# Block operands of a Strassen-Winograd up projection: stored ready for use, or made from stored h where they are used

## The chip, the cores and the metric

The kernel runs on one core of one Trainium2 chip. The metric is the device time of one execution in microseconds (us), the median of several runs. Five instruction streams work side by side and meet at semaphores: TensorE (PE, matmuls), VectorE (DVE), ScalarE (ACT), GpSimd (POOL) and SyncE (SP). SP and POOL here also issue the transfers between HBM and on-chip memory, each as a queue of its own in order of issue.

## The reference

One decoder layer on 2048 tokens of width 1024, all in fp32:

```
u   = x @ W_in                         # columns q | k | v | rnn-x | rnn-gate
att = sliding_window_attention(q, k, v, sinks)
rec = rg_lru(causal_conv(rnn-x)) * gelu(rnn-gate)
h   = LN1(alpha * x + concat(att, rec) @ W_out)
g, v = split(h @ W_up)                 # 2 x 3072 columns
ffn = (gelu(causal_conv3(g)) * v) @ W_down
ple = sigmoid(h @ W_g + b_g) * (p @ W_p)
out = LN2(alpha * h + ffn + ple)
```

## The kernel before

Every fp32 factor of a matmul is split into a high and a low half in a type that PE multiplies at a higher rate: ACT casts the high half and DVE subtracts it (`split_sb`, L122 to L124), and `mm3` (L140 to L143) sums three matmuls, high·high, high·low and low·high. Weights come as 512 KB blocks by SP into three buffers (wst) and are split into eight buffers of a pair of halves (wb). Transposed activations lie in 13 buffers of 1 MB (pool h).

The first part loops over four chunks c of 512 tokens. The input stage projects x (halves xh, xl) and runs attention and the recurrence. The gate stage is the output projection (`mh`, `ml`), LN1, transposes of h into halves hh, hl and an fp32 copy hf (L517 to L526), and the per-layer gate: small products of p (halves in `pt`, bank `a`) and the product h W_g (bank `acc`), put together by DVE and ACT (L588 to L592), and the row sums stored to `rsd` (L594).

The second part runs twice, s2 = 0 and 1, over a pair of chunks: `up(s2)` and `down(s2)`. up multiplies the 1024-wide h of both chunks with the up weights as a 2x2 block product by the Strassen-Winograd scheme: seven products in place of eight for each of 24 weight tiles ft. h's four blocks are B11 (chunk 2·s2, first 512 features), B21 (the same chunk, last 512), B12 and B22 (the next chunk). The operands are B11, T2 = B22 − B12 + B11, B21, T1 = B12 − B11, T3 = B22 − B12, T4 = B21 − T2 and B22, each as a high and a low half of four quarters kt. `begin(ft)` splits seven weight combinations and multiplies B11; `middle` does T2, B21 (which completes the gate block of the first chunk), T1 and T3; `end` does T4 and B22. PE's order in up is the order in the code; elsewhere a scheduler sets the order of all engines.

The operands go through HBM. In chunks 0 and 2 the halves of B11 and B21 are stored as they are (L537) beside fp32 hf (L538). In chunks 1 and 3, between the token blocks of the gate, `combine(kt)` (L543 to L557) fetches a quarter of B11 and B21 by SP into two rows of pool xb (L546, L547), makes the four sums on DVE (L549 to L552), splits them into pch and pcl, and stores the halves to hxT2, hxT1, hxT3, hxT4 by POOL (L556, L557). `load_hx` (L238 to L251) loads finished operands by POOL: for s2 = 0 in chunk 3 (L529, L600), for s2 = 1 in down(0) (L753, L772). xb has two buffers, which up also uses for the convolution rows (L653, L675).

x is loaded by SP through the wst buffers (L275 to L284), and so are the row constants (`load_rows`, L206).

Of the kernel before, what the change touches and what calls it, by code (L numbers as in the profile page):

```python
# [8 lines left out]
F32 = mybir.dt.float32  # L9
# [19 lines left out]
HX = ("B11", "T2", "B21", "T1", "T3", "T4", "B22")  # L29
# [11 lines left out]
def kernel(  # L41
# [196 lines left out]
    def load_hx(s2, names, earlier):  # L238

        for n in names:  # L240
            hx[s2][n] = []
            for m in range(2):
                if (n, m) == (HX[-1], 1):
                    ts = [tm(("pch", "pcl")[k % 2], F32R) for k in range(4)]
                    for k in range(4):
                        order(POOL.dma_start(f(ts[k]), hxd[s2][n][:, m, k, :]), earlier)
                else:
                    t = h8(n, [P, 4, T])
                    order(POOL.dma_start(f(t), hxd[s2][n][:, m]), earlier)
                    ts = [t[:, k, :] for k in range(4)]  # L250
                hx[s2][n].append(ts)  # L251

    for c in range(NCH):
# [21 lines left out]
        for u in range(c == 0, 4):  # L275
            if c == 0:
                st = tm("r", cols=1024)
            else:
                st = wst_p.tile([P, 1024], F32, tag="wst", name=nm("wst"))
            order(SP.dma_start(st.rearrange("p (k t) -> p k t", k=2), xt[c, :, 2 * u:2 * u + 2, :]), have_h)  # L280
            hi, lo = x_flat(u)
            for h in range(2 - (c > 0)):
                hs = slice(h * 512, 1024 if c else h * 512 + 512)
                split_sb(st[:, hs], hi[:, hs], lo[:, hs])  # L284
# [570 lines left out]
```

## Time and profile before

| | |
|---|---|
| median of 3 runs | 2374.26 us (2372.97 to 2375.92) |
| profiled execution | 2377.13 us, its span 2375.4 us |
| mean granted clock of PE | 0.987 of 2.4 GHz |
| PE busy | 2291.5 us, 96% of the span |
| DVE, ACT, POOL busy | 1653.0, 1084.5, 265.2 us |
| packets of SP's queue, of POOL's | 266.97 MB and 71.31 MB |

The span is the time from the first instruction to the last on the chip; the time of the execution is a little longer. Busy time says how long an engine worked, not whether the end waited for it. In a timeline row the brackets hold how long the engine stood idle before this instruction, and the instruction or the transfer that released it. In a row of windows, the number in brackets behind a busy time is the count of instructions, then follow the granted clock (1.00 is 2.4 GHz, 0.50 is 1.2 GHz), the share of time in which the core's transfer engines worked, and what they moved.

### The profile page before, as it was taken

How to read it: one execution, taken by the hardware profiler on the slowest of the kernel's cores; microseconds unless marked ns; L12 is line 12 of the kernel's file. 1: busy time of each engine (PE TensorE's matmuls, PEld its weight loads, DVE VectorE, ACT ScalarE, POOL GpSimd, SP SyncE). 2: the span in 40 equal slices, each digit the busy share in tenths (PEclk: the TensorE clock that was granted, in tenths of full speed). 3: DMA queues.
4: the chain of work that ended last, by engine and by line, in shares of the span. 5: the costliest groups of instructions: out<-in, count | busy, mean ns of one | idle time of the engine just before them, and what ended most of it. 6: DMA issues, size and time to landing. Idle time of an engine off the chain costs nothing.

```text
span 2375.4 us, 28589 instructions
## 1 busy us (share of the span) xinstructions
PE 2291.5 (96%) x10156; PEld 1871.1 (79%) x10156; DVE 1653.0 (70%) x2728; ACT 1084.5 (46%) x2030; POOL 265.2 (11%) x483
## 2 busy tenths in 40 slices
PE   8899999899999977999999999999999999999998
PEld 7777777677787756888888888878888888888886
DVE  6975787778778756777777753636877777753735
ACT  7644664566456443444444433333444444433331
POOL 0300130213003112001001000000000000000000
PEclk9999999999999988999999999999999999999999
DMA  4237324832542468222222264765322222254542
GB/s 161 98 108 262 119 80 168 293 115 74 213 165 90 170 238 326 85 80 87 87 80 82 92 208 133 271 238 201 117 86 80 85 80 83 90 193 153 194 158 83
DMA packets 102095, 340.11 MB, mean 143 GB/s; under 512 B 10944, under 2 KB 11072, under 8 KB 96576
## 3 DMA queue, kind: packets, MB, share of 16 engines
q1 hardware_dynamic: 87840, 266.97, 33.9%
q0 software_dynamic: 14112, 71.31, 7.6%
q8 instruction: 80, 1.31, 0.2%
q14 instruction: 63, 0.52, 0.1%
HBM read 262.74 MB, written 75.50 MB: 142 GB/s over the span
## 4 chain that ended last, share of the span: by engine, by line
PE 59%; DVE 2%; DMA 1%; ACT 0%; issue 0%; DVEq 0%; ACTq 0%
PE b L141 7%; PE b L143 7%; PE b L142 7%; PE acc L141 5%; PE acc L143 5%; PE acc L142 5%; PE a L141 5%; PE a L143 5%; PE a L142 5%; PE sc L143 2%; PE sc L142 2%; PE sc L141 2%; DMA wst<-in_w_dram 1%; DMA xb<-hfd 0%; DVE st L214 0%
## 5 line engine op out<-in xcount | busy, mean ns | idle before, releaser
L123 ACT CAST wb<-wst 128x512 fp32r<-128x512 f32 x640 | 391.9, 622 | 677.0 <-PE acc L143 321.3
L124 DVE TENSOR_TENSOR wb<-wst,wb 128x512 fp32r<-128x512 f32 x640 | 433.5, 686 | 277.4 <-ACT wb L123 276.6
L141 PE MATMUL b<-T,wb 128*128 128x512 f32 x576 | 225.5, 392 | 7.1 <-DMA T<-hxT 5.4
L142 PE MATMUL b<-T,wb 128*128 128x512 f32 x576 | 225.2, 391 | 1.9 <-DMA T<-hxT 1.9
L143 PE MATMUL b<-T,wb 128*128 128x512 f32 x576 | 225.1, 391 | 0.0
L123 ACT CAST wb<-xc 128x512 fp32r<-128x512 f32 x144 | 89.4, 621 | 199.1 <-PE a L143 94.5
L141 PE MATMUL a<-B,wb 128*128 128x512 f32 x384 | 149.6, 390 | 0.0
L142 PE MATMUL a<-B,wb 128*128 128x512 f32 x384 | 149.5, 389 | 0.0
L143 PE MATMUL a<-B,wb 128*128 128x512 f32 x384 | 149.4, 389 | 0.0
L124 DVE TENSOR_TENSOR wb<-xc,wb 128x512 fp32r<-128x512 f32 x144 | 99.1, 688 | 50.8 <-ACT wb L123 50.8
L141 PEld LDWEIGHTS b<-T,wb 128*128 128x128 f32 x576 | 108.6, 189 | 31.1 <-issue 5.8
L142 PEld LDWEIGHTS b<-T,wb 128*128 128x128 f32 x576 | 108.6, 189 | 24.9 <-DMA T<-hxT 2.4
L620 DVE SCALAR_TENSOR_TENSOR pl<-xb,prm,pl 128x512 f32<-128x512 f32 x96 | 71.8, 748 | 78.7 <-POOL xb L676 77.4
L143 PEld LDWEIGHTS b<-T,wb 128*128 128x128 f32 x576 | 108.7, 189 | 22.7
L141 PE MATMUL acc<-wb,hh 128*128 128x512 f32 x256 | 101.5, 401 | 11.4 <-DVE P L588 5.8
L143 PE MATMUL acc<-wb,hl 128*128 128x512 f32 x256 | 101.7, 399 | 1.7 <-DVE hl L99 1.7
L142 PE MATMUL acc<-wb,hh 128*128 128x512 f32 x256 | 102.3, 400 | 0.0
L142 PE MATMUL a<-xl,wb 128*128 128x512 f32 x256 | 101.0, 394 | 0.0
L141 PE MATMUL a<-xh,wb 128*128 128x512 f32 x256 | 100.7, 393 | 0.0
L143 PE MATMUL a<-xh,wb 128*128 128x512 f32 x256 | 100.6, 393 | 0.0
L141 PE MATMUL acc<-xh,wb 128*128 128x512 f32 x192 | 77.5, 403 | 8.0 <-ACT wb L123 7.5
L143 PEld LDWEIGHTS a<-B,wb 128*128 128x128 f32 x384 | 72.2, 188 | 15.1
(272 smaller groups left out, 5728.0 us busy)
## 6 DMA issues: line engine op xcount, KB each, us to landing
wst<-in_w_dram SPq DMA_DIRECT2D x319, 512.0 KB, 3.6
graw<-gd SPq DMA_DIRECT2D x24, 1024.0 KB, 6.4
T<-hxT POOLq DMA_DIRECT2D x16, 1024.0 KB, 9.8
gd<-pl SPq DMA_DIRECT2D x48, 256.0 KB, 2.0
gd<-r SPq DMA_DIRECT2D x48, 256.0 KB, 4.2
B<-hxB POOLq DMA_DIRECT2D x10, 1024.0 KB, 9.7
r<-in_xn_dram SPq DMA_DIRECT2D x16, 512.0 KB, 4.0
ln<-in_rows_dram SPq DMA_DIRECT2D x16, 512.0 KB, 4.5
```

What stands on the lines that cost most here:

```text
L123: ACT.copy(hi, src)
L124: (eng or DVE).tensor_tensor(lo, src, f(hi), ALU.subtract)
L141: order(PE.matmul(o, ah, bh, start=first, stop=False, skip_group_check=more), after)
L142: PE.matmul(o, ah, bl, start=False, stop=False, skip_group_check=more)
L143: return PE.matmul(o, al, bh, start=False, stop=last, skip_group_check=more)
L620: DVE.scalar_tensor_tensor(gc, xb[:, t_:t_ + T], pc(C_FW + 3 * ft + t_), gc, ALU.mult, ALU.add)
```

## The change

HBM keeps only hf, in fp32, as two halves of 1 MB for each of the four chunks. The operands are made where they are used. `combine(0, kt)` now runs in chunk 3's gate alone: POOL fetches a quarter of B11 (into an xb row), B12 (pch) and B22 (pcl); the split goes straight to tiles of pool h, which now stay. `combine(1, kt)` runs in down(0)'s second chunk. At the start of each up, `combine_b21` makes B21 and T4 from a fetched quarter and from T2's halves, and `combine_b22` makes B22. For the first tile the product with B21 stands behind those with T1 and T3. x is loaded by POOL as two tiles of 1 MB in pool h, and the row constants by POOL too. Lines of the changed kernel differ from those above.

```diff
-    hfd = [scratch(f"hfd{s}", [P, 8, T], F32) for s in range(2)]
+    hfd = [[scratch(f"hf{c}_{u}", [P, 4, T], F32) for u in range(2)] for c in range(NCH)]
     gd = [[scratch(f"gd{s}_{k}", [P, 4, 2 * T], F32) for k in range(NF // 4)] for s in range(2)]
-    hxd = [{n: scratch(f"hx{n}_{s}", [P, 2, 4, T], F32) for n in HX} for s in range(2)]
 
     def load_rows(i):
         t = tm("ln", cols=1024)
-        SP.dma_start(t, rows[i:i + 1].broadcast_to([P, 1024]))
+        POOL.dma_start(t, rows[i:i + 1].broadcast_to([P, 1024]))
...
-    def load_hx(s2, names, earlier):
...
+    def fetch(t, c, u, kt, earlier):
+        order(POOL.dma_start(t, hfd[c][u][:, kt, :]), earlier)
+        return t
+
+    def operands(s2, names):
         for n in names:
-            hx[s2][n] = []
-            for m in range(2):
-                if (n, m) == (HX[-1], 1):
-                    ts = [tm(("pch", "pcl")[k % 2], F32R) for k in range(4)]
-                    for k in range(4):
-                        order(POOL.dma_start(f(ts[k]), hxd[s2][n][:, m, k, :]), earlier)
-                else:
-                    t = h8(n, [P, 4, T])
-                    order(POOL.dma_start(f(t), hxd[s2][n][:, m]), earlier)
-                    ts = [t[:, k, :] for k in range(4)]
-                hx[s2][n].append(ts)
+            hx[s2][n] = [[t[:, k, :] for k in range(4)] for t in (h8(n, [P, 4, T]), h8(n, [P, 4, T]))]
+
+    def operand(s2, n, kt, src):
+        split_sb(src, hx[s2][n][0][kt], hx[s2][n][1][kt])
+
+    def combine(s2, kt, earlier):
+
+        if kt == 0:
+            operands(s2, ("B11", "T2", "T1", "T3"))
+        b11 = fetch(row()[:, 0:T], 2 * s2, 0, kt, earlier)
+        b12 = fetch(tm("pch"), 2 * s2 + 1, 0, kt, earlier)
+        b22 = fetch(tm("pcl"), 2 * s2 + 1, 1, kt, earlier)
+        t3, t1, t2 = (tm("xc") for _ in range(3))
+        DVE.tensor_tensor(t3, b22, b12, ALU.subtract)
+        operand(s2, "B11", kt, b11)
+        DVE.tensor_tensor(t2, t3, b11, ALU.add)
+        operand(s2, "T2", kt, t2)
+        DVE.tensor_tensor(t1, b12, b11, ALU.subtract)
+        operand(s2, "T1", kt, t1)
+        operand(s2, "T3", kt, t3)
+
+    def combine_b21(s2, kt, earlier):
+
+        if kt == 0:
+            operands(s2, ("B21", "T4"))
+        b21 = fetch(row()[:, 0:T], 2 * s2, 1, kt, earlier)
+        operand(s2, "B21", kt, b21)
+        t4 = tm("xd")
+        DVE.tensor_tensor(t4, f(hx[s2]["T2"][0][kt]), f(hx[s2]["T2"][1][kt]), ALU.add)
+        DVE.tensor_tensor(t4, b21, t4, ALU.subtract)
+        operand(s2, "T4", kt, t4)
+
+    def combine_b22(s2, earlier):
+        hi = h8("B22", [P, 4, T])
+        hx[s2]["B22"] = [[hi[:, k, :] for k in range(4)], [tm(("pch", "pcl")[k % 2], F32R) for k in range(4)]]
+        for kt in range(4):
+            operand(s2, "B22", kt, fetch(row()[:, 0:T], 2 * s2 + 1, 1, kt, earlier))
...
+        if c > 0:
+            for u in range(2):
+                st = h8("xs", [P, 4, T], F32)
+                order(POOL.dma_start(st, xt[c, :, 4 * u:4 * u + 4, :]), have_h)
+                for h in range(2):
+                    hi, lo = x_flat(2 * u + h)
+                    split_sb(st[:, 2 * h:2 * h + 2, :].rearrange("p k t -> p (k t)"), hi, lo)
...
-        if c == NCH - 1:
-            load_hx(0, HX[:1], last_scores)
-            load_hx(0, HX[1:3], [mixed])
...
-        if c % 2 == 0:
-            for u, n in enumerate(("B11", "B21")):
-                for m, t in enumerate((hh_[u], hl_[u])):
-                    POOL.dma_start(hxd[s2][n][:, m], f(t))
-                POOL.dma_start(hfd[s2][:, 4 * u:4 * u + 4], hf[u])
-        else:
-            for m, t in enumerate((hh_[1], hl_[1])):
-                POOL.dma_start(hxd[s2]["B22"][:, m], f(t))
-
...
-            SP.dma_start(b11, hfd[s2][:, kt, :])
-            SP.dma_start(b21, hfd[s2][:, 4 + kt, :])
-            t3, t1, t2, t4 = (tm(t) for t in ("xc", "xc", "xc", "xd"))
-            DVE.tensor_tensor(t3, b22, b12, ALU.subtract)
-            DVE.tensor_tensor(t1, b12, b11, ALU.subtract)
-            DVE.tensor_tensor(t2, t3, b11, ALU.add)
-            DVE.tensor_tensor(t4, b21, t2, ALU.subtract)
-            for n, t in (("T2", t2), ("T1", t1), ("T3", t3), ("T4", t4)):
-                hi, lo = tm("pch", F32R), tm("pcl", F32R)
-                split_sb(t, hi, lo)
-                POOL.dma_start(hxd[s2][n][:, 0, kt, :], f(hi))
-                POOL.dma_start(hxd[s2][n][:, 1, kt, :], f(lo))
+        for u in range(2):
+            POOL.dma_start(hfd[c][u], hf[u])
...
-                if c % 2 and t_ % 2 != dh:
-                    combine(2 * dh + t_ // 2)
-            if dh == 0:
-                half = [gated]
-        if c == NCH - 1:
-            load_hx(0, HX[3:6], half)
-            load_hx(0, HX[6:], [gated])
+                if c == NCH - 1 and t_ % 2 != dh:
+                    combine(0, 2 * dh + t_ // 2, last_scores)
+            ready_for_b21 = [gated]
...
+            def gate():
+                product(v["A"], w2, x["B21"], False)
...
+            if not first:
+                gate()
             product(v["C"], w5, x["T1"], True)
             product(v["B"], w7, x["T3"], False)
...
+            if first:
+                gate()
...
             v = begin(0)
-            middle(v)
+            for kt in range(4):
+                combine_b21(s2, kt, ready_for_b21)
+            middle(v, True)
+            combine_b22(s2, ready_for_b21)
...
+                if c == 1 and 3 < kp < 8:
+                    combine(1, kp - 4, marks[-1:])
...
-                    if c == 1:
-                        load_hx(1, HX[:4], marks[-1:])
...
-            if c == 1:
-                load_hx(1, HX[4:], marks[-2:-1])
...
-        down(s2)
+        ready_for_b21 = down(s2)
```

Three places show how instructions move. The first is POOL at the seam between chunk 3's gate and up(0). Before: rsd15 is the last row-sum store of the gate, the hx names are operands in HBM, gtail a small copy of the first tile's convolution.

```order
291 L594 DMA rsd15_117<-r_1363_7249 128x1024
292 L249 DMA T3_1553_8202<-hxT3_0_136 128x2048
293 L249 DMA T3_1554_8204<-hxT3_0_136 128x2048
294 L249 DMA T4_1555_8206<-hxT4_0_137 128x2048
295 L249 DMA T4_1556_8208<-hxT4_0_137 128x2048
296 L249 DMA B22_1557_8210<-hxB22_0_138 128x2048
297 L246 DMA pch_1558_8212<-hxB22_0_138 128x512
298 L246 DMA pcl_1559_8213<-hxB22_0_138 128x512
299 L246 DMA pch_1560_8214<-hxB22_0_138 128x512
300 L246 DMA pcl_1561_8215<-hxB22_0_138 128x512
301 L654 COPY xb_1579_8297<-gtail_100 128x2
```

After, from the last rsd stores on; hf0_1 is the second half of chunk 0's h in HBM (B21), hf1_1 that of chunk 1 (B22), ln a row constant.

```order
238 L237 DMA pch_1452_7909<-hf1_0_120 128x512
239 L598 DMA rsd12_114<-r_1298_7071 128x1024
240 L598 DMA rsd13_115<-r_1299_7073 128x1024
241 L598 DMA rsd14_116<-r_1300_7075 128x1024
242 L237 DMA xb_1477_8011<-hf0_1_119 128x512
243 L237 DMA xb_1479_8020<-hf0_1_119 128x512
244 L206 DMA ln_2057_11648<-in_rows_dram 128x1024
245 L598 DMA rsd15_117<-r_1301_7077 128x1024
246 L237 DMA xb_1481_8029<-hf0_1_119 128x512
247 L237 DMA xb_1483_8038<-hf0_1_119 128x512
248 L656 COPY xb_1490_8103<-gtail_100 128x2
249 L658 COPY gtail_100<-xb_1490_8103 128x2
```

Nine loads of whole operands and quarters behind the last rsd store are gone. Eight fetches of a quarter stand there instead, each into an xb row; two of them ahead of the last rsd store, four behind the small copies of the first tile.

The second place is DVE at the start of up(0). Before, the first tile's weight combinations (wb, wst, xc) follow the gate's last operations on row sums (P, r); ph is the first sum behind a product with T2.

```order
1244 L592 SCALAR_TENSOR_TENSOR r_1363_7249<-r_1363_7249,P_1550_8192 128x512
1245 L124 TENSOR_TENSOR wb_1570_8240<-xc_1564_8226,wb_1570_8240 128x512
1246 L633 TENSOR_TENSOR wst_1563_8224<-wst_1562_8222,wst_1563_8224 128x512
1247 L636 TENSOR_TENSOR xc_1566_8228<-wst_1562_8222,xc_1565_8227 128x512
1248 L651 TENSOR_TENSOR ph_1578_8283<-b_1576_8269,P_1575_8267 128x512
1249 L124 TENSOR_TENSOR wb_1571_8244<-wst_1563_8224,wb_1571_8244 128x512
1250 L124 TENSOR_TENSOR wb_1572_8247<-wst_1563_8224,wb_1572_8247 128x512
1251 L124 TENSOR_TENSOR wb_1573_8251<-xc_1566_8228,wb_1573_8251 128x512
1252 L124 TENSOR_TENSOR wb_1588_8342<-wst_1583_8334,wb_1588_8342 128x512
1253 L627 TENSOR_TENSOR xc_1585_8338<-wst_1584_8336 128x512
```

After, from the first B21 split on; B21 and T4 rows with L123 are low halves, L270 and L271 the sums for T4, and wb_1506 and up are weights of the second tile.

```order
1216 L123 TENSOR_TENSOR B21_1474_8008<-xb_1477_8011,B21_1473_8007 128x512
1217 L271 TENSOR_TENSOR xd_1478_8015<-xb_1477_8011,xd_1478_8015 128x512
1218 L123 TENSOR_TENSOR B21_1474_8008<-xb_1479_8020,B21_1473_8007 128x512
1219 L651 TENSOR_TENSOR ph_1487_8061<-b_1485_8047,P_1472_8005 128x512
1220 L123 TENSOR_TENSOR T4_1476_8010<-xd_1478_8015,T4_1475_8009 128x512
1221 L123 TENSOR_TENSOR wb_1506_8141<-wst_1501_8133,wb_1506_8141 128x512
1222 L270 TENSOR_TENSOR xd_1480_8024<-T2_1394_7612,T2_1395_7613 128x512
1223 L629 TENSOR_TENSOR xc_1504_8138<-xc_1503_8137,wst_1501_8133 128x512
1224 L271 TENSOR_TENSOR xd_1480_8024<-xb_1479_8020,xd_1480_8024 128x512
1225 L123 TENSOR_TENSOR B21_1474_8008<-xb_1481_8029,B21_1473_8007 128x512
1226 L123 TENSOR_TENSOR wb_1507_8145<-xc_1504_8138,wb_1507_8145 128x512
1227 L123 TENSOR_TENSOR T4_1476_8010<-xd_1480_8024,T4_1475_8009 128x512
```

Splits and sums of B21 and T4 now stand between the weights of the second tile, and in DVE's order a weight waits behind a quarter that is still to be fetched.

The third place is POOL in chunk 0's gate. Before, six stores of operands and hf, and then the stores of row sums, the next small copy behind them in the program's later part:

```order
58 L537 DMA hxB11_0_132<-hh_274_1603 128x2048
59 L537 DMA hxB11_0_132<-hl_276_1605 128x2048
60 L538 DMA hfd0_118<-hf_278_1607 128x2048
61 L537 DMA hxB21_0_134<-hh_275_1604 128x2048
62 L537 DMA hxB21_0_134<-hl_277_1606 128x2048
63 L538 DMA hfd0_118<-hf_279_1608 128x2048
64 L594 DMA rsd0_102<-r_236_1319 128x1024
65 L594 DMA rsd1_103<-r_237_1321 128x1024
```

After, with the loads of the next chunk's x (xs) and of row constants:

```order
59 L206 DMA ln_241_1321<-in_rows_dram 128x1024
60 L206 DMA ln_300_1707<-in_rows_dram 128x1024
61 L313 DMA xs_369_2114<-in_xt_dram 128x2048
62 L561 DMA hf0_0_118<-hf_278_1599 128x2048
63 L561 DMA hf0_1_119<-hf_279_1600 128x2048
64 L313 DMA xs_370_2120<-in_xt_dram 128x2048
65 L598 DMA rsd0_102<-r_236_1311 128x1024
```

Four stores went, two stores of hf stay, and the second half of x stands behind them on the same queue.

## Rows read from the trace of the kernel before

**Rows 1.** The page's first part: busy us, share of the span, instructions of each engine

```profile
PE 2291.5 (96%) x10156; PEld 1871.1 (79%) x10156; DVE 1653.0 (70%) x2728; ACT 1084.5 (46%) x2030; POOL 265.2 (11%) x483
```

**Rows 2.** Windows by stage: stretch, us, busy us by engine, clock, DMA share, GB/s

```profile
335.23:453.45 118.22, 110.04 (x482) 86.36 (x480) 93.15 (x141) 61.55 (x106) 23.93 (x44) 0.99 0.57 200
453.45:564.06 110.61, 102.20 (x477) 82.77 (x477) 91.24 (x183) 73.19 (x176) 26.65 (x40) 0.97 0.39 129
564.06:674.41 110.35, 107.38 (x481) 85.76 (x480) 79.69 (x118) 55.99 (x95) 11.07 (x19) 1.00 0.51 179
674.41:779.23 104.82, 100.06 (x477) 81.35 (x476) 85.99 (x169) 70.48 (x170) 24.76 (x36) 1.00 0.35 115
779.23:915.07 135.84, 116.66 (x482) 90.80 (x481) 92.84 (x143) 57.92 (x102) 27.30 (x50) 0.91 0.62 232
915.07:1385.49 470.42, 461.80 (x2021) 380.90 (x2020) 344.82 (x537) 197.07 (x323) 47.40 (x110) 0.99 0.33 107
1385.49:1647.68 262.19, 260.88 (x1150) 215.23 (x1148) 126.22 (x196) 84.68 (x149) 9.18 (x17) 1.00 0.59 210
1647.68:2106.26 458.58, 458.16 (x2022) 379.05 (x2021) 348.21 (x541) 195.65 (x320) 34.29 (x72) 1.00 0.30 99
```

**Rows 3.** PE timeline, gate stage of chunk 3: start, us, instruction, [idle before, releaser]

```profile
838.87 0.79 PE L141 MATMUL acc<-wb,hh 128*128 128x512 f32 x1 [4.53 <-ACT wb L123]
...
853.62 0.79 PE L141 MATMUL a<-wb,pt 128*128 128x512 f32 x1 [4.73 <-ACT pt L123]
...
858.49 0.79 PE L143 MATMUL a<-wb,pt 128*128 128x512 f32 x1 [3.65 <-DVE pt L124]
...
907.86 0.50 PE L141 MATMUL acc<-wb,hh 128*128 128x512 f32 x1 [3.55 <-DVE P L588]
```

**Rows 4.** DVE timeline, same stage

```profile
856.61 0.69 DVE L550 TENSOR_TENSOR xc<-hf,xb 128x512 f32<-128x512 f32 x1 [2.51 <-DMA xb<-hfd]
...
903.98 0.69 DVE L550 TENSOR_TENSOR xc<-hf,xb 128x512 f32<-128x512 f32 x1 [6.45 <-DMA xb<-hfd]
```

**Rows 5.** PE timeline, start of chunk 2's input stage

```profile
453.45 0.50 PE L141 MATMUL acc<-xh,wb 128*128 128x512 f32 x1 [2.14 <-ACT wb L123]
...
458.01 0.80 PE L143 MATMUL acc<-xh,wb 128*128 128x512 f32 x1 [3.83 <-DVE wb L124]
```

**Rows 6.** PE timeline, start of up(0)

```profile
931.49 0.77 PE L141 MATMUL b<-T,wb 128*128 128x512 f32 x1 [5.38 <-DMA T<-hxT]
...
943.62 0.50 PE L141 MATMUL b<-T,wb 128*128 128x512 f32 x1 [1.33 <-DVE xd L662]
```

**Rows 7.** Windows: late gate of chunk 3, start of up(0), start of up(1)

```profile
828.21:915.07 86.86, 68.58 (x274) 52.64 (x273) 55.61 (x88) 37.51 (x67) 19.54 (x37) 0.86 0.73 273
915.07:945.00 29.93, 21.30 (x79) 16.42 (x78) 16.61 (x28) 10.53 (x19) 8.76 (x17) 0.83 0.92 356
1647.68:1672.00 24.32, 24.32 (x109) 20.15 (x108) 23.80 (x39) 11.18 (x19) 1.83 (x4) 1.00 0.59 220
```

**Rows 8.** Groups by line: line, engine, operation, count, busy us, mean ns, idle before

```profile
L124 DVE TENSOR_TENSOR wb<-wst,wb 128x512 fp32r<-128x512 f32 x640 | 433.5, 686 | 277.4 <-ACT wb L123 276.6
...
L123 ACT CAST wb<-wst 128x512 fp32r<-128x512 f32 x640 | 391.9, 622 | 677.0 <-PE acc L143 321.3 <-PE b L143 192.3 <-DMA wst<-in_w_dram 70.0
...
L556 POOL DMA_DIRECT2D hxT<-pch x32 | 17.2, 540 | 58.0 <-ACT pch L123 57.8
```

**Rows 9.** DMA issues: name, queue, count, KB each, median us to landing

```profile
hxT<-pch POOLq DMA_DIRECT2D x32, 256.0 KB, 4.7
...
wst<-in_xt_dram SPq DMA_DIRECT2D x12, 512.0 KB, 4.3
...
hfd<-hf POOLq DMA_DIRECT2D x4, 1024.0 KB, 14.5
...
xb<-hfd SPq DMA_DIRECT2D x16, 256.0 KB, 5.8
...
pch<-hxB POOLq DMA_DIRECT2D x4, 256.0 KB, 12.2
```

More of the change, by code (lines that the diff above doesn't have):

```diff
@@ L27 @@
 EPS = 1e-5
-HX = ("B11", "T2", "B21", "T1", "T3", "T4", "B22")
 W_IN, W_OUT, W_UP, W_DOWN, W_PG, W_PP = 0, 14, 22, 70, 94, 102
@@ L274 @@
                 ready[W_IN + 6].append(wblock(st[1][:, hs]))
-        for u in range(c == 0, 4):
+        for u in range(1, 4):
             if c == 0:
                 st = tm("r", cols=1024)
-            else:
[L279 to L284, printed above, removed]
+                SP.dma_start(st.rearrange("p (k t) -> p k t", k=2), xt[c, :, 2 * u:2 * u + 2, :])
+                hi, lo = x_flat(u)
+                for h in range(2):
+                    hs = slice(h * 512, h * 512 + 512)
+                    split_sb(st[:, hs], hi[:, hs], lo[:, hs])
+        if c > 0:
+            for u in range(2):
+                st = h8("xs", [P, 4, T], F32)
+                order(POOL.dma_start(st, xt[c, :, 4 * u:4 * u + 4, :]), have_h)
+                for h in range(2):
+                    hi, lo = x_flat(2 * u + h)
+                    split_sb(st[:, 2 * h:2 * h + 2, :].rearrange("p k t -> p (k t)"), hi, lo)
         def first_stage(o, unit, bh, bl):
@@ L526 @@
                 ACT.copy(hf[u][:, :, t_ * P:(t_ + 1) * P], tpv)
-        if c == NCH - 1:
-            load_hx(0, HX[:1], last_scores)
-            load_hx(0, HX[1:3], [mixed])
-        s2 = c // 2
-        if c % 2 == 0:
-            for u, n in enumerate(("B11", "B21")):
-                for m, t in enumerate((hh_[u], hl_[u])):
-                    POOL.dma_start(hxd[s2][n][:, m], f(t))
-                POOL.dma_start(hfd[s2][:, 4 * u:4 * u + 4], hf[u])
-        else:
-            for m, t in enumerate((hh_[1], hl_[1])):
-                POOL.dma_start(hxd[s2]["B22"][:, m], f(t))
-        def combine(kt):
-            b12, b22 = hf[0][:, kt, :], hf[1][:, kt, :]
-            b11, b21 = row()[:, 0:T], row()[:, 0:T]
-            SP.dma_start(b11, hfd[s2][:, kt, :])
-            SP.dma_start(b21, hfd[s2][:, 4 + kt, :])
-            t3, t1, t2, t4 = (tm(t) for t in ("xc", "xc", "xc", "xd"))
-            DVE.tensor_tensor(t3, b22, b12, ALU.subtract)
-            DVE.tensor_tensor(t1, b12, b11, ALU.subtract)
-            DVE.tensor_tensor(t2, t3, b11, ALU.add)
-            DVE.tensor_tensor(t4, b21, t2, ALU.subtract)
-            for n, t in (("T2", t2), ("T1", t1), ("T3", t3), ("T4", t4)):
-                hi, lo = tm("pch", F32R), tm("pcl", F32R)
-                split_sb(t, hi, lo)
-                POOL.dma_start(hxd[s2][n][:, 0, kt, :], f(hi))
-                POOL.dma_start(hxd[s2][n][:, 1, kt, :], f(lo))
+        for u in range(2):
+            POOL.dma_start(hfd[c][u], hf[u])
         fence()
@@ L643, in begin, with middle @@
             return v
-        def middle(v):
+        def middle(v, first=False):
             ft, (w1, w2, w3, w4, w5, w6, w7) = v["ft"], v["w"]
@@ L651, in middle @@
             DVE.tensor_tensor(v["u2"], v["B"], p1, ALU.add)
-            product(v["A"], w2, x["B21"], False)
-            xb = row()
-            POOL.tensor_copy(xb[:, 0:2], gtail[:, ft, :])
-            ACT.copy(xb[:, 2:2 + T], v["A"])
-            POOL.tensor_copy(gtail[:, ft, :], xb[:, T:T + 2])
-            v["gc"] = tm("pl")
-            conv(v["gc"], v["A"], xb, ft)
+            def gate():
+                product(v["A"], w2, x["B21"], False)
+                xb = row()
+                POOL.tensor_copy(xb[:, 0:2], gtail[:, ft, :])
+                ACT.copy(xb[:, 2:2 + T], v["A"])
+                POOL.tensor_copy(gtail[:, ft, :], xb[:, T:T + 2])
+                v["gc"] = tm("pl")
+                conv(v["gc"], v["A"], xb, ft)
+            if not first:
+                gate()
             product(v["C"], w5, x["T1"], True)
@@ L779, in down @@
                 later.append(rest)
+        return marks[-2:-1]
     for s2 in range(2):
         up(s2)
-        down(s2)
+        ready_for_b21 = down(s2)
 _INS = ["xt", "xn", "pt", "w", "gw", "par", "rows", "sinks"]
```

## The prediction

> **What bounds the kernel now.** I read first the busy times of the engines: TensorE (PE) is busy 2291.5 of a span of 2375.4 us [rows 1]. The product count does not change, so at most some 84 us of PE idle time, and what half clock costs, can be won. Second came the windows, cut at the first matmul of each stage [rows 2]. Here the reader should compare stages that do equal work. The gate stage (out projection, first norm, per-layer gate) takes 110.35 us in chunk 2, 118.22 in chunk 1 and 135.84 in chunk 3, with PE busy 107.38, 110.04 and 116.66 us. The input and attention stage takes 104.82 in chunk 3, but 110.61 in chunk 2, right behind the gate of chunk 1. Chunks 1 and 3 are the ones that call combine in the gate. So the price of combine can be read as 118.22 − 110.35 = 7.9 us, 110.61 − 104.82 = 5.8 us and 135.84 − 110.35 = 25.5 us. Third, PE's own timeline says how: in chunk 3 PE stands 4.53, 4.73, 3.65 and 3.55 us for weights wb, the two halves of pt and a psum bank that DVE empties (P), which ScalarE (ACT) and VectorE (DVE) have ready late [rows 3]; the granted clock of the stage is 0.91, a mix of the two levels 2.4 and 1.2 GHz, after these stops. At those moments DVE itself stands in order behind a combine row that a DMA still brings, 2.51 and 6.45 us [rows 4]. Behind chunk 1's gate PE waits 2.14 and 3.83 us for weight splits [rows 5]. The first up projection, up(0), stops 5.38 us for a T operand (T3 by its place) and 1.33 us for DVE [rows 6], and is 470.42 us where up(1) is 458.58 [rows 2].
>
> **The change part by part.**
>
> *Combine leaves chunk 1's gate.* Four calls go, each with 4 additions and 4 splits on DVE and ACT, 8 stores on POOL and 2 fetches on SP. Removed from DVE there: 4 × 8 × 0.69 us, the mean of a split's low half, = 22 us, and from ACT 4 × 4 × 0.62 = 10 us [rows 8]. What remains is what chunk 2's gate does, so I take its time, 110.35: −8 us. Of the stops behind it, 2.14 + 3.83 = 5.97 us, I take all: chunk 2's input stage comes to 104.8, −6 us. Both ends: nothing, if something else holds the weights there, and −14 as taken.
>
> *Chunk 3's gate.* It keeps a combine, now for the first pair. Counted per call: before 4 additions and 4 low halves on DVE, 4 high halves on ACT; after, 3 additions and 4 low halves on DVE, 4 high halves on ACT. DVE has thus 28 instructions in place of 32, hardly less. What goes is the in-order standing: before, half of combine's rows were fetched inside the gate and the 8 stores per call had to free the two pch and pcl buffers before the next split (DVE busy was only 55.61 of 86.86 us, with DMA at 0.73 [rows 7]). After, POOL fetches the first two b11 rows ahead of the gate, splits go straight into tiles that stay, and 32 stores of 256 KB and the loads of B11, T2, B21, T1, T3, T4, B22 (seven operands of two halves of 1 MB) are gone. What is late next: the halves of T3 reuse the h tiles of hf, so they wait until chunk 3's own hf store has landed (14.5 us [rows 9], issued at the stage's middle, before the last calls), and psum banks of the first small products wait for ACT, 2 to 3 us. I take chunk 2's 110.35 plus 2.5: about 112.8, −23 us. The ends: −10 if half of the stops stay, −25.5 if none do.
>
> *up(0).* One product of the up projection is 458.16 / 24 / 7 = 2.73 us of PE [rows 2]. Let E be the first matmul of the stage. Before, all operands were loads that POOL queued behind stores and weights; it cost 11.84 us against up(1). After, B21 and T4 are made from four fetches through two xb rows, and B22 from four more through the same two rows. The gate product was moved behind T1 and T3, so B21 is wanted at E + 4 × 2.73 = E + 10.9 for its first quarter and near E + 13 for the last, and B22 at E + 19.1. On POOL three rsd stores stand ahead of the first two b21 fetches, and a load of row constants and the fourth rsd store, which waits for DVE's last addition of the gate, ahead of the other two. With a landing of L a round through two rows costs 2 × 0.54 us issue, L, and splits of about 1.3 us, say L + 1.9. The two rounds of B21 can begin some 5 us before E: late by 2(L + 1.9) − 18 us. The two rounds of B22 begin when the gate product ends, some 5.5 us ahead of need, which itself spreads over a product: late by 2(L + 1.9) − 8. For L I have hxT stores of 256 KB at 4.7, xb fetches at 5.8, and pch at 12.2 us [rows 9]; the last stood in a stretch in which DMA was 0.92 busy at 356 GB/s [rows 7], most of it the operand loads that the change removes, so I take 4 to 5. Then B22 stops PE 4 to 6 us; B21's last quarter, behind DVE's queue, 2 to 3; together about 9, and some 3 us at the lower clock after such stops, as before. 457.6 + 12 = 470: change 0, between −8 (L = 3, all early) and +10.
>
> *The skill's DMA fit.* The trace has 256 KB at 4.7 and 5.8 us [rows 9]. The Trainium skill, "DMA: Bandwidth & Descriptors", section "Anatomy of one DMA — SWDGE (gpsimd) path", gives a fixed 2.0 us plus bytes over 436 GB/s, an estimate of 2.6 us for such a fetch; by it B22 would be late by 1 us only and up(0) would end near 462.
>
> *down(0)* takes combine(1): 28 DVE instructions of 0.69, 19 us, in a stage where DVE is busy 126.22 of 262.19 us: nothing; if its cover failed, at most a few stops of a us or two.
>
> *up(1)* loses its ready operands. In the first 24.32 us of it PE never stood, and DVE was busy 23.80 us [rows 7]. The change adds 4 × 4 instructions for B21 and T4 and 4 for B22, 20 × 0.69 = 14 us of DVE [rows 8]. Some of B21 and T4 can be made ahead of E; weights of the next tile stand behind the rest. I take +10, between +3 (all but B22 ahead) and +18.
>
> *x and row constants on POOL's queue.* x was 512 KB through the wst buffers with 4.3 us [rows 9]; now two 1 MB loads go into h tiles. The second stands on POOL behind the stores of hf, which wait for ACT's copies, but a whole input stage's lead is left in chunks 0 to 2. Taken as 0; if it is late, the split of x's second half stops PE by up to 5 us a chunk.
>
> *Sum:* −8 − 6 − 23 + 0 + 0 + 10 = −27. The profiled execution took 2377.13 us (1.73 beyond its span), so 2350.1; it lies 2.87 above the median 2374.26, so the median becomes about **2347 us**.
>
> **The rivals.**
>
> *Slow start (slower).* Each up starts with B21 and B22 made in rounds of two rows at the loaded landing, L = 12.2. Then B21 is late by 28 − 18 = 10 us and B22 by 28 − 8 = 20, 30 for each up, 60 together in place of the 9 to 12 of up(0)'s own old stall and of 0 in up(1): 60 − 12 = +48 against −37 of the other stages: about +11, 2385. It decides from the sum 4L − 18.4 per up where two of them less the old 12 reach 37, L = 10.7. For it: the pch row in the same place of the program. Against: the traffic that slowed it is gone.
>
> *Half gain.* The gate of chunk 3 is held not by stores and fetches but by the sheer ACT and DVE work, of which 28 of 32 instructions stay. Then −10 there, and the sum is −14: 2360. For it: DVE's count. Against: in the 86.86 us DVE was idle 31 of them [rows 7].
>
> *Blocked POOL queue.* POOL's issues of combine's stores took 540 ns in the mean [rows 8], in gates where DVE was busy for more than two thirds of the time [rows 2]. The Trainium skill, "SBUF — State Buffer", section "SBUF: two separate sides", warns that a DMA issued from GpSimd cannot have its descriptors written while DVE runs a two-port mode. This would make x and the fetches late on the queue to which the change moves them. As a mechanism of this kernel: each of four rounds per up held for one DVE instruction more, 0.69 us, and x's loads for some 1 us: 2 × 4 × 0.69 + 4 = about +10, 2357. Those short issues speak against it.
>
> *It does nothing:* if the stops of chunk 3 move to up(0) in full, −14 + 10 = about −4: 2370.
>
> **How the numbers follow.** Forecast 0.60, half gain 0.17, blocked queue 0.05, does nothing 0.08, slow start 0.10. The forecast's own range, from its terms, is −8 − 6 − 25.5 − 8 + 3 = −44.5 at the best and −8 − 6 − 15 + 7 + 10 = −12 at the worst, 2330 to 2362. To hold eight in ten I go up to the half gain and part of the fourth case: 2329 to 2371. A change under 0.2% (4.7 us) cannot be told from none by these runs. Faster takes the forecast, the half gain, the blocked queue and part of the fourth, 0.84; same, part of the fourth and the mild end of the slow start, 0.07; slower 0.09.
>
> **What would show it.** Chunk 1's gate and chunk 2's input stage should come to within 2 us of 110 and 105. In chunk 3's gate the stops of 4.5 us for wb and pt should be gone and DVE should not stand behind a fetched row for over 3 us. In up(0) the only stops should be before the first gate product and the first B22 product, the fetches landing in 3 to 6 us. up(1) should show stops in its first 30 us, where it had none. I am wrong if up(1) loses over 20 us, if landings of the fetches are near 10 us, or if an input stage opens with PE waiting for x's second half.

## The result and the profile after

The changed kernel takes 2349.33 us (2346.03 to 2350.27, 4 runs) beside 2374.51 (2372.97 to 2375.92, 4 runs): 0.9892 of the time before, 95% interval 0.9874 to 0.9909. The forecast was 2347 us. The span of the profiled execution falls from 2375.4 to 2348.1 us. The first part of the page, to hold against [rows 1]:

```profile
PE 2288.0 (97%) x10156; PEld 1869.3 (80%) x10156; DVE 1670.4 (71%) x2760; ACT 1096.4 (47%) x2054; POOL 252.0 (11%) x439
```

PE lost 3.5 us of busy time and 24 us of idle time. The windows, cut as in [rows 2] at the first matmul of each stage (gate stages of chunks 0 and 1, input stage of chunk 2, gate stages of chunks 2 and 3, up(0), down(0), up(1); columns as there):

```profile
118.66:225.69 107.03, 105.31 (x473) 84.86 (x472) 76.84 (x115) 53.20 (x92) 9.64 (x16) 1.00 0.41 144
330.32:438.98 108.66, 107.33 (x482) 85.78 (x480) 79.28 (x118) 55.63 (x95) 11.62 (x20) 1.00 0.41 144
438.98:544.73 105.75, 101.33 (x477) 82.65 (x476) 86.30 (x175) 70.24 (x170) 24.63 (x36) 0.98 0.34 112
544.73:653.34 108.61, 107.29 (x481) 85.78 (x480) 79.23 (x118) 55.52 (x95) 11.59 (x20) 1.00 0.43 144
759.38:869.38 110.00, 107.30 (x482) 85.77 (x480) 93.19 (x146) 60.18 (x108) 16.62 (x30) 1.00 0.47 154
869.38:1342.02 472.64, 464.42 (x2022) 381.70 (x2021) 352.45 (x550) 200.36 (x329) 51.16 (x105) 0.99 0.30 95
1342.02:1608.68 266.66, 263.52 (x1149) 217.16 (x1148) 148.18 (x232) 95.43 (x169) 8.47 (x16) 0.99 0.51 173
1608.68:2079.00 470.32, 463.03 (x2021) 380.61 (x2020) 355.39 (x553) 200.77 (x328) 42.75 (x79) 0.99 0.30 95
```

Chunk 1's gate is 9.6 us shorter, the input stage behind it 4.9, chunk 3's gate 25.8, at a granted clock of 1.00 where it was 0.91. Chunk 2's gate is 1.7 us shorter and chunk 0's 5.8 (from 112.83). On the other side up(0) is 2.2 us longer, down(0) 4.5 and up(1) 11.7. The stages not shown differ by at most 1.2 us. With all of them the sum is −27.3, as the spans say. (In three further runs of the kernel before, shown below, chunk 0's gate took 108.2 to 111.9 us and up(0) 469.4 to 472.5, so part of the first gain may be spread, and all of up(0)'s loss; up(1) took 458.5 to 459.2 there and down(0) 262.1 to 262.4.)

None of the four stops of [rows 3] is left; the longest in chunk 3's gate is 1.14 us. The new stops of PE are in up(0), down(0) and up(1), each row with its idle time and releaser in brackets:

```profile
878.83 0.47 PE L140 MATMUL b<-T,wb 128*128 128x512 f32 x1 [1.13 <-DVE ph L651]
...
886.10 0.50 PE L140 MATMUL a<-B,wb 128*128 128x512 f32 x1 [2.20 <-ACT B L122]
887.73 0.80 PE L141 MATMUL a<-B,wb 128*128 128x512 f32 x1 [1.13 <-DVE B L123]
...
897.11 0.79 PE L140 MATMUL b<-T,wb 128*128 128x512 f32 x1 [3.15 <-DVE xd L667]
...
1528.86 0.80 PE L140 MATMUL sc<-wb,gb 128*128 128x512 f32 x1 [2.63 <-ACT gb L726]
...
1626.57 0.50 PE L140 MATMUL b<-T,wb 128*128 128x512 f32 x1 [1.41 <-DVE xd L667]
...
1633.12 0.50 PE L140 MATMUL acc<-B,wb 128*128 128x512 f32 x1 [2.58 <-ACT B L122]
...
1639.18 0.79 PE L140 MATMUL acc<-B,wb 128*128 128x512 f32 x1 [3.08 <-ACT B L122]
```

In up(0) the first row is the product with T3, the next two are the last quarter of B21 and the fourth is the product with T4, 7.6 us in all. The product with B22 stopped PE there for 0.4 us only (0.16 at 903.22, 0.22 at 903.95). In up(1) the three rows are the product with T4 and two quarters of B22. The 5.38 us of [rows 6] for a loaded operand has become several stops of 1 to 3 us, and up(1) has the like. In up(0), whose first matmul is at 869.38, POOL's rows are:

```profile
868.58 0.53 POOL L598 DMA_DIRECT2D rsd<-r  x1 [5.76 <-DVE r L596]
869.11 1.08 POOL L237 DMA_DIRECT2D xb<-hf  x2
...
878.00 0.54 POOL L237 DMA_DIRECT2D xb<-hf  x1 [2.72 <-DVE xd L271]
...
892.08 0.54 POOL L237 DMA_DIRECT2D xb<-hf  x1 [1.94 <-DVE xd L271]
```

The first two fetches of B21 went out 0.3 us before the first matmul, behind a store of row sums that had waited for DVE. The third (878.00) and the first of B22 (892.08) each waited for L271, the subtraction that makes T4 and reads the row last. At the start of up(1), whose first matmul is at 1608.68, this is plainer:

```profile
1614.88 0.54 POOL L237 DMA_DIRECT2D xb<-hf  x1 [28.69 <-DVE xd L271]
...
1619.44 5.24 POOL L656 COPY xb<-gtail 128x2 f32<-128x2 f32 x1
...
1625.24 0.54 POOL L237 DMA_DIRECT2D xb<-hf  x1
...
1634.09 0.54 POOL L237 DMA_DIRECT2D xb<-hf  x1 [3.51 <-DVE pcl L123]
```

The first row is the last B21 fetch (the other three went out by 1585.65). POOL stood 28.69 us before it, for L271 of the second quarter, which still read the row and which DVE did at 1613.67:

```profile
1613.67 0.69 DVE L271 TENSOR_TENSOR xd<-xb,xd 128x512 f32<-128x512 f32 x1
```

The fetches of B22 follow at 1625 to 1634 (two of four are shown), the last of them 6.3 us after 1608.68 + 19.1, when its product was due. The landings were short beside the 4.7 to 12.2 us that [rows 9] has for transfers of 256 KB (KB each, median us to landing):

```profile
xs<-in_xt_dram POOLq DMA_DIRECT2D x6, 1024.0 KB, 8.2
...
xb<-hf POOLq DMA_DIRECT2D x24, 256.0 KB, 3.7
```

### The profile page after: what moved, and what is told of

Read it like the earlier page. It is cut to its first block, busy times and chain, and to the rows that moved or that the text cites. A ratio compares the mean times of both kernels' runs of the same rounds, so it can differ in the third digit from the quotient of the medians.

```text
span 2348.1 us, 28409 instructions
## 1 busy us (share of the span) xinstructions
PE 2288.0 (97%) x10156; PEld 1869.3 (80%) x10156; DVE 1670.4 (71%) x2760; ACT 1096.4 (47%) x2054; POOL 252.0 (11%) x439
## 4 chain that ended last, share of the span: by engine, by line
PE 82%; DVE 10%; ACT 3%; issue 3%; DMA 2%; POOL 0%; SPq 0%; ACTq 0%; POOLq 0%; DVEq 0%
PE acc L142 10%; PE acc L141 10%; PE acc L140 9%; PE a L142 8%; PE a L140 8%; PE a L141 8%; PE b L140 7%; PE b L141 7%; PE b L142 7%; PE sc L142 2%; PE sc L141 2%; PE sc L140 2%; DVE wb L123 1%; DMA xb<-hf 1%; ACT P L118 1%
## 5 line engine op out<-in xcount | busy, mean ns | idle before, releaser
L123 DVE TENSOR_TENSOR wb<-wst,wb 128x512 fp32r<-128x512 f32 x640 | 434.1, 686 | 261.2 <-ACT wb L122 260.4
L123 DVE TENSOR_TENSOR wb<-xc,wb 128x512 fp32r<-128x512 f32 x144 | 99.0, 688 | 52.1 <-ACT wb L122 52.1
L140 PEld LDWEIGHTS a<-B,wb 128*128 128x128 f32 x384 | 72.7, 189 | 17.8 <-ACT B L122 2.6
L141 PEld LDWEIGHTS a<-B,wb 128*128 128x128 f32 x384 | 72.7, 189 | 16.7 <-DVE B L123 1.6
```

The source lines that it names most:

```text
L123: (eng or DVE).tensor_tensor(lo, src, f(hi), ALU.subtract)
L140: order(PE.matmul(o, ah, bh, start=first, stop=False, skip_group_check=more), after)
L141: PE.matmul(o, ah, bl, start=False, stop=False, skip_group_check=more)
```

## The experiments

Each experiment is one profiled execution, but for two that were timed several times (the wider fetches with the gate product second, and the norms later). So stages are compared and not totals: the first input stage alone varied between 110.1 and 113.8 us over these runs. In the three runs of the changed kernel whose edits leave the up projections alone (the first below, the stores of chunks 0 and 2, and combine(1) spread), up(0) took 470.9 to 473.4 us and up(1) 468.4 to 469.8, beside 472.64 and 470.32 in the change. So a difference of about 2 us in one run's up is spread.

**x and row constants on SP again.**

```diff
-        POOL.dma_start(t, rows[i:i + 1].broadcast_to([P, 1024]))
+        SP.dma_start(t, rows[i:i + 1].broadcast_to([P, 1024]))
...
-                order(POOL.dma_start(st, xt[c, :, 4 * u:4 * u + 4, :]), have_h)
+                order(SP.dma_start(st, xt[c, :, 4 * u:4 * u + 4, :]), have_h)
```

> The changed kernel with row constants and x on SP's queue again, ahead of and between the weights there. Theory A (as predicted, the queue is worth nothing): stages within 1.5 us of the changed kernel's (gates 107.0, 108.7, 108.6, 110.0; input stages 104.6, 105.8, 106.0), total 2349 +- 3. Rival B (the 5.8 us that chunk 0's gate gained, which was not forecast, came from x leaving the weights' queue): chunk 0's gate goes back to 110 to 113, and total is 2354 to 2360.

2353.19 us. All stages are within 1.5 us but one, chunk 1's gate:

```profile
330.53:441.95 111.42, 108.33 (x481) 85.57 (x480) 79.45 (x118) 55.60 (x95) 8.97 (x15) 1.00 0.43 140
```

It is 2.8 us longer here, with small stops, the longest of 0.92 us for a weight split, and so outside theory A's 1.5 us. Chunk 0's gate is 106.95, so rival B falls. The queue is worth 0 to 3 us.

**No fetches at the start of up.** `b21` and `b22` are read from T3's quarter on the chip.

```diff
-        b21 = fetch(row()[:, 0:T], 2 * s2, 1, kt, earlier)
+        b21 = f(hx[s2]["T3"][0][kt])
...
-            operand(s2, "B22", kt, fetch(row()[:, 0:T], 2 * s2 + 1, 1, kt, earlier))
+            operand(s2, "B22", kt, f(hx[s2]["T3"][0][kt]))
```

> The changed kernel with B21 and B22 not fetched: their splits read a quarter of T3 that is on the chip already. DVE and ACT work is the same, the values are not the operands'. Theory W (an up start is paid by VectorE's 20 extra instructions in order): up(0) 468 to 473 and up(1) 467 to 471, as now (472.6 and 470.3). Rival F (by rounds of fetches through two rows): up(0) and up(1) fall by 5 to 8 us each, to 464 to 467 and 462 to 465.

up(0) and up(1), whole stages:

```profile
867.28:1327.90 460.62, 458.97 (x2022) 378.94 (x2021) 350.73 (x548) 197.90 (x325) 40.50 (x96) 1.00 0.29 93
...
1594.98:2056.86 461.88, 459.01 (x2021) 378.82 (x2020) 354.04 (x552) 199.26 (x327) 35.29 (x73) 1.00 0.30 94
```

−12.0 and −8.4 us with the same DVE work: theory W as stated falls, and F gained more than it said. DVE is no less busy at these starts (22.69 of the first 22.72 us of up(0), 23.83 of the first 25.02 of up(1)). But with the data at hand the splits come sooner: the last of them stands 16.7 and 14.6 us after the stage's first matmul, where the change has 35.0 and 30.5.

**Fetches without DVE work.** ACT copies make both halves of B21, T4 and B22.

```diff
-        operand(s2, "B21", kt, b21)
+        for m in range(2):
+            ACT.copy(hx[s2]["B21"][m][kt], b21)
...
-        operand(s2, "T4", kt, t4)
+        for m in range(2):
+            ACT.copy(hx[s2]["T4"][m][kt], b21)
```

> The changed kernel with the fetches kept, but B21, T4 and B22 made by ScalarE copies alone (both halves a copy of the fetched quarter, T4 too): 20 VectorE instructions less at each up start, 12 ScalarE copies more. Theory W: up(1) falls to 459 to 463 (from 470.3), up(0) to 463 to 467 (from 472.6). Rival F: both stay within 2 us.

```profile
869.84:1341.71 471.87, 464.24 (x2021) 380.92 (x2020) 341.45 (x531) 206.17 (x341) 42.36 (x105) 0.99 0.31 95
...
1606.71:2072.75 466.04, 461.03 (x2022) 380.46 (x2020) 346.93 (x537) 204.94 (x337) 29.35 (x79) 0.99 0.31 96
```

up(0) −0.8, which is within the spread, and up(1) −4.3. W's ranges (463 to 467 and 459 to 463) are missed, and so is F's for up(1). What stays in up(1) is the wait for B22:

```profile
1628.93 0.50 PE L140 MATMUL acc<-B,wb 128*128 128x512 f32 x1 [1.67 <-ACT B L279]
...
1633.52 0.80 PE L140 MATMUL acc<-B,wb 128*128 128x512 f32 x1 [3.32 <-ACT B L279]
```

So the fetches through two rows are the larger part in both. DVE's queue is a second one in up(1), and holds the rows there: without its work the last B21 fetch went out 1.0 us after the stage's first matmul in place of 6.2. (The run also has 12 more ACT copies at each start, so it is no clean measure of DVE's share.)

**The gate product at its old place.**

```diff
-            middle(v, True)
+            middle(v)
```

> The changed kernel with the first tile's gate product at its old place, second after T2, so that B21 is wanted 5.5 us earlier. If B21 is what is late at the start (both theories), up(0) gets 4 to 6 us longer, to 477 to 479, and up(1) 3 to 6 longer. If B21 is in time and only B22 late, no change within 1.5 us.

```profile
868.40:1340.75 472.35, 464.31 (x2021) 380.80 (x2020) 352.82 (x550) 200.76 (x329) 43.12 (x105) 0.99 0.30 95
...
1606.81:2072.11 465.30, 461.06 (x2022) 379.93 (x2021) 355.09 (x553) 200.86 (x328) 39.67 (x79) 1.00 0.30 96
```

up(0) −0.3 and up(1) −5.0, where both theories had both longer; the other case, no change, holds for up(0) alone. The later gate product of the change costs 3 to 5 us in up(1), given the spread. The times of the fetches fit that: the small copies of that product stand ahead of B22's fetches on POOL, and its row is one of the two. At the old place B22's first two fetches went out at 1622.10 and 1622.99, 15.3 and 16.2 us after the stage's first matmul, where the change has 16.6 and 19.0, and the last at 23.1 in place of 25.4. That these are the whole cause is argued, not shown.

**The stores of chunks 0 and 2 put back.**

```diff
+        if c % 2 == 0:
+            for u in range(2):
+                for m, t in enumerate((hh_[u], hl_[u])):
+                    POOL.dma_start(scratch(f"hx{c}{u}{m}", [P, 4, T], F32), f(t))
+                POOL.dma_start(hfd[c][u], hf[u])
```

> The changed kernel with the four stores of h's halves (1 MB each) that chunks 0 and 2 made before, back on POOL's queue ahead of hf, into memory that nothing reads. Theory S (the stores were what delayed chunk 0's gate: weights and p landed late beside them): chunk 0's gate goes from 107.0 back to 110 to 113 and chunk 2's from 108.6 to 110 to 111. Rival (x's way through the weights' buffers did it, as both kernels' stores are hidden): both stay within 1 us.

Gates of chunks 0 and 2:

```profile
117.54:231.45 113.91, 106.93 (x473) 86.03 (x472) 77.31 (x115) 53.37 (x92) 11.78 (x20) 0.97 0.46 172
...
551.82:667.46 115.64, 109.77 (x481) 87.45 (x480) 79.81 (x118) 55.91 (x95) 13.74 (x24) 0.97 0.46 171
```

+6.9 and +7.0 us, more than theory S expected, each with a stop where PE waits for ACT to empty the bank of a small product. ACT in its turn, in chunk 0's gate, stood for a weight (its row last); in chunk 2's it stood 4.56 us for one:

```profile
205.25 0.79 PE L140 MATMUL a<-wb,pt 128*128 128x512 f32 x1 [5.88 <-ACT ph L587]
...
640.53 0.79 PE L140 MATMUL a<-wb,pt 128*128 128x512 f32 x1 [4.54 <-ACT ph L587]
```

```profile
204.10 0.62 ACT L122 CAST wb<-wst 128x512 fp32r<-128x512 f32 x1 [5.89 <-DMA wst<-in_w_dram]
```

With six stores in one stretch, and both loads of x pushed behind them on POOL (180.70 and 189.33, where the change has 172.80 and 185.53), the weights on SP's queue land late: 7 us a chunk. The run does not part the stores from the later loads of x. And 7 us is not what the stores cost in the kernel before: there the same six stood in chunk 2's gate, with x on SP's queue, the stop at this place was 1.66 us, and the stage took 110.35. In three further runs of the kernel before, with edits in chunk 3 alone, chunk 0's gate took 108.2, 110.8 and 111.9 us and chunk 2's 110.0 to 110.3: of the 5.8 us that chunk 0 gained, 1 to 5 are left beside these runs, and the rest is the spread of the kernel before.

**Chunk 3's gate: no stores, no fetches, no combine.** Three edits of the kernel before. The first:

```diff
-                POOL.dma_start(hxd[s2][n][:, 0, kt, :], f(hi))
-                POOL.dma_start(hxd[s2][n][:, 1, kt, :], f(lo))
+                if c < 3:
+                    POOL.dma_start(hxd[s2][n][:, 0, kt, :], f(hi))
+                    POOL.dma_start(hxd[s2][n][:, 1, kt, :], f(lo))
```

> The kernel before with combine's 32 stores left out in chunk 3 (the second pair's T operands are then the first pair's, so the values differ). Theory S3 (the last gate was held by pch and pcl, which come free only when the stores have landed): chunk 3's gate falls from 135.8 to 113 to 120. Rival F3 (by the fetches that DVE stands behind in order): it stays at 128 to 136. Rival H (by DVE's and ACT's own work): 128 to 136 here and in the run without fetches.

```profile
781.24:911.55 130.31, 114.17 (x481) 89.52 (x480) 96.96 (x150) 62.06 (x108) 14.37 (x25) 0.92 0.55 197
```

The second:

```diff
+            if c < 3:
+                SP.dma_start(b11, hfd[s2][:, kt, :])
+                SP.dma_start(b21, hfd[s2][:, 4 + kt, :])
+            else:
+                b11, b21 = hf[0][:, kt, :], hf[1][:, kt, :]
```

> The kernel before with combine's 8 fetches left out in chunk 3, the sums made of rows of h on the chip, so the values differ. Theory S3: chunk 3's gate stays at 130 to 136. Rival F3: it falls to 113 to 122, as DVE's two stops of 2.5 and 6.5 us and what they cost PE's clock go. Rival H: 130 to 136.

```profile
781.28:908.63 127.35, 115.48 (x481) 89.63 (x480) 92.41 (x143) 59.02 (x104) 27.72 (x50) 0.93 0.59 224
```

The third:

```diff
-                if c % 2 and t_ % 2 != dh:
+                if c == 1 and t_ % 2 != dh:
                     combine(2 * dh + t_ // 2)
```

> The kernel before with combine left out of chunk 3 altogether: no fetches, sums, splits or stores there (the second pair's T operands are the first pair's, so the values differ). The loads of the first pair's operands into chunk 3's gate and the two stores of B22's halves stay. If the loads and stores of whole operands share the blame with combine (the stop of 4.5 us for weights at the stage's start stood behind three 1 MB loads), the gate stays at 116 to 124 us and that stop stays. If combine alone holds the gate, it falls to 110 to 113.

```profile
775.28:895.23 119.95, 111.20 (x482) 87.40 (x480) 77.63 (x118) 52.97 (x92) 14.24 (x25) 0.97 0.53 196
```

From 135.84: −5.5 without stores, −8.5 without fetches, −15.9 without any of combine. S3 falls, 127.35 lies outside all three ranges, and the third run comes out where loads and stores share the blame. So neither the stores nor the fetches alone are the cause, and 120 is 10 us above the changed kernel's 110.0. What remained is the stop near the start of the product with h (the expectation calls it the stage's start), 4.53 us in [rows 3]:

```profile
835.05 0.79 PE L141 MATMUL acc<-wb,hh 128*128 128x512 f32 x1 [4.68 <-ACT wb L123]
```

Before that stop this run issues three loads of finished operands of 1 MB at 821.74 to 824.46, and ACT stood 5.02 us for the weight that was loaded beside them (in the kernel before 825.72 to 828.44, and 4.86 us). The loads and B22's stores were not taken out alone, so that they are these 10 us is argued, not shown.

**combine(1) spread.**

```diff
-                if c == 1 and 3 < kp < 8:
-                    combine(1, kp - 4, marks[-1:])
+                if c == 1 and kp in (2, 4, 6, 8):
+                    combine(1, kp // 2 - 1, marks[-1:])
```

> The changed kernel with combine(1) spread over weight pairs 2, 4, 6 and 8 of down(0)'s second chunk in place of 4 to 7. If the 2.63 us stop of PE for a gb split and the clock after it are what cost down(0) 4.5 us, and come from two users of ACT in neighbouring pairs, down(0) falls from 266.7 to 262 to 264. If one call of combine in a pair is enough for the stop, it stays at 266 to 267.

down(0) took 267.3 us, as one call in a pair would have it, and the stop is there once, behind the first call wherever it stands:

```profile
1507.14 0.50 PE L140 MATMUL sc<-wb,gb 128*128 128x512 f32 x1 [2.63 <-ACT gb L726]
```

The other three calls cost PE no stop of 0.4 us or more. That the first call, which takes eight of the 13 tiles of pool h, shortens the lead of the gb splits fits this, but was not tried.

**Wider fetches.** B21 (and B22 for the first pair) in two transfers of 512 KB into r tiles, with the gate product second or last.

```diff
+        if kt % 2 == 0:
+            pair[:] = [tm("r", cols=1024).rearrange("p (k t) -> p k t", k=2)]
+            order(POOL.dma_start(pair[0], hfd[2 * s2][1][:, kt:kt + 2, :]), earlier)
+        b21 = pair[0][:, kt % 2, :]
```

> The changed kernel with B21 fetched as two transfers of 512 KB into row-sum tiles (r) in place of four through the two xb rows, for the first pair B22 as well, and with the first tile's gate product at its old place. Theory F (rounds through two rows set the up starts; the run without fetches gave 460.6 and 461.9): up(0) 463 to 468 and up(1) 460 to 464, total 2333 to 2342. Rival W (the 20 VectorE instructions): up(0) 470 to 473, up(1) 464 to 466 as with the gate product at its old place alone.

> The same fetches as the other version, but with the first tile's gate product behind T1 and T3, as in the changed kernel. If its later place only helped to bridge late fetches and costs by itself (it frees its xb row and bank later), up(1) is 2 to 5 us longer than in the other version and up(0) equal within 2. If B21 is still late there, it is shorter instead.

Gate second: 2346.74 us, 0.9873 of the time before [0.9857, 0.9890]; up(0) 471.5, in the range of rival W, and up(1) 469.9, above both ranges. Gate last, one run: 2343.12. Its up(0) and up(1), and the first 35 us of up(1):

```profile
869.58:1338.79 469.21, 461.75 (x2022) 381.09 (x2020) 352.33 (x550) 200.34 (x329) 57.53 (x100) 0.99 0.30 96
...
1604.65:2072.23 467.58, 460.38 (x2022) 380.23 (x2020) 357.53 (x557) 201.26 (x330) 48.61 (x76) 0.99 0.29 95
...
1604.70:1640.00 35.30, 28.36 (x118) 22.99 (x117) 33.84 (x56) 17.32 (x29) 4.44 (x8) 0.90 0.43 152
```

up(1) is not the 460 to 464 of theory F: PE stands for a weight split of the second tile, and DVE was busy 33.84 of 35.30 us.

```profile
1625.81 0.80 PE L142 MATMUL a<-B,wb 128*128 128x512 f32 x1 [6.94 <-DVE wb L123]
```

With B21 early, its splits, those of T4 and B22 and the norms of down(0)'s last two token blocks went ahead of the second tile's weights. So F alone fails as well; the start is set by rows and DVE's order together. The expectation on the gate's place also failed: last is 2.3 and 2.4 us shorter here, about as much as the spread.

**Norms later.** Wider fetches for the first pair only, the gate product last there and second for the other pair, and:

```diff
             v = begin(0)
...
-            while later:
-                later.pop(0)()
             for ft in range(1, NF):
...
                 middle(v)
+                if ft == 2:
+                    while later:
+                        later.pop(0)()
```

> The changed kernel with three edits: for the first pair B21 and B22 come as 512 KB transfers into row-sum tiles (r); for the second pair they come through the two xb rows as now, but the first tile's gate product keeps its old second place; and the second norm of the last two token blocks of down(0), which VectorE did in the first tile of up(1), comes after the second tile's middle. Theory FW (an up start is set by fetches through two rows and by VectorE's queue together; in the two versions with wider fetches up(1) still stood 7 to 9 us for a weight split behind norms and B22): up(0) 467 to 469, up(1) 459 to 463, total 2335 to 2342. Rival F (rounds alone): the norms are worth nothing and up(1) is 465 to 467, as in the run with the gate product at its old place, total 2340 to 2345.

2340.34 us (2335.64 to 2340.91, 5 runs), 0.9840 of the kernel before [0.9826, 0.9855], clear of the change's 0.9892 [0.9874, 0.9909].

```profile
869.84:1339.64 469.80, 462.04 (x2022) 381.40 (x2020) 352.64 (x550) 200.59 (x329) 56.98 (x100) 0.99 0.30 96
...
1605.64:2069.89 464.25, 459.81 (x2021) 378.78 (x2020) 354.82 (x553) 200.66 (x328) 42.14 (x79) 1.00 0.31 96
```

up(0) −2.8 and up(1) −6.1 us against the change; up(0) lies 0.8 us above its range. But up(1) with 464.25 lies between the two expectations, and the gate product's old place alone had given 465.3: how much the norms are worth, 1 us or none, stays open.

## Why the prediction held, and where not

The sum was −27 and the spans give −27.3. That is better than its terms were, and in part luck.

- Chunk 1's gate and chunk 2's input stage: −8 and −6 forecast, −9.6 and −4.9 measured. The comparison with stages of equal work carried: chunk 1's gate takes 108.66 us and chunk 2's 108.61.
- Chunk 3's gate: −23 forecast, −25.8 measured, and 1.4 us above chunk 2's gate where 2.5 were allowed. The prediction took combine's stores and fetches and the loads of operands as one price. The runs part them: without all of combine 15.9 us go, and that the other 10 are the loads and B22's stores is argued. The rival of half gain falls: DVE is busy 93.19 us there as it was 92.84, and the stage still takes 110.
- up(0): 0 forecast, +2.2 measured. The size was right by luck. The prediction had B22 stop PE for 4 to 6 us, and it stopped PE 0.4; B21's last quarter, forecast at 2 to 3, took 3.3; T4 and T3, for which it had nothing, took 3.15 and 1.13. Its sign that PE would stop only before B21 and B22 failed. (Its base of 457.6 is not in the rows either; up(1) before was 458.58, which makes the sum 470.6.)
- The steps of that term that failed are the start and the round. The first round was to begin 5 us before the first matmul, and began 0.3 us before it. A round was to cost L + 1.9, with L the landing: 8.3 us for B21 in up(0), where the first fetch landed in 6.4, and 5.4 for B22, where it landed in 3.45. They took 8.9 (869.11 to 878.00) and 7.1 (892.08 to 899.14), and in up(1) the last B21 fetch went out 29.2 us after the one before it. The rows did not come free at the rate of landings, since T4's subtraction and the splits held them in DVE's queue.
- up(1): +10 forecast, +11.7 measured, 7.3 us of stops and the rest the lower clock after them. The prediction expected the weights of the next tile to stand behind the new DVE work; what PE stood for was T4 (1.41) and B22 (2.58 and 3.08). The runs show fetches and DVE's order together behind it.
- The Trainium skill, "DMA: Bandwidth & Descriptors", section "Anatomy of one DMA — SWDGE (gpsimd) path", gave the estimate of 2.6 us for such a fetch. The shortest measured was 3.1, with the 0.54 us of the issuing instruction in it, and up(0) took not 462 us but 472.6.
- down(0): nothing forecast, +4.5 measured, one stop of 2.63 us, 0.51 behind it, and the lower clock after it. DVE's and ACT's spare time was there; the order behind the first call was not looked at.
- Chunks 0 and 2: no term at all, −7.5 measured. The list of removed work left out their four stores. By the other runs of the kernel before, 1 to 6 us of chunk 0 and 1.4 to 1.7 of chunk 2 are the change's; how much of it is the stores and how much x's new way is open, since the run that put the stores back moved x's loads as well. This missing gain and the missing loss in down(0) nearly cancel, and so the sum came out.
- The slow start did not come: the fetches at the starts of up landed in 3.1 to 6.6 us, not 12.2. The blocked POOL queue did not either: x landed in 8.2 us for 1 MB, and the run with x and rows on SP was not faster.
- The stated range was narrower than its terms: its worst case took −15 for chunk 3's gate, +7 for up(0) and +10 for up(1), where the terms themselves ended at −10, +10 and +18.

## What to carry to other kernels

Data that must pass through two small buffers can be paced by the last reader of a buffer and not by the transfer: look for that reader in the order of its engine. Price what a change takes away in every stage in which it stood, stores too, since a store that nobody waits for can go with a late load that somebody waits for, as in the run with the stores put back. When a late operand is bridged by a reordering, check what else the moved product held: here its row and its place on the queue.

## Not expected of the hardware

With four more stores of 1 MB on POOL's queue and the loads of x behind them, ACT stood 5.89 and 4.56 us for a weight on SP's queue, and the two gates were 7 us longer, the lower clock after the stop included.

A copy of 128x2 elements on POOL was recorded as 5.24 us at 1619.44, where DVE had no idle time. In two other runs with the same code there it took 5.34 and 5.24 us, in the run with the stores put back 0.67. Most copies of this kind in up took 0.18 to 0.6 us, ten took 2.39. It is not what made up(1) late: in the run with 0.67 us the fetches of B22 went out 16.2, 19.3, 21.4 and 25.4 us after the first matmul, as in the change within 0.4 us, and up(1) took 468.4.
